# Two column blocks of the latent branch's output projection as a pair with seven-product units, and the last sums in another place

## The chip, the cores and the metric

The kernel runs on one core of one Trainium2 chip. The metric is the time of one execution in device microseconds (us). Five engines work side by side, each through its own queue of instructions, in order: TensorE (PE, matmuls), VectorE (DVE), ScalarE (ACT), GpSimd (POOL) and SyncE (SP). SP and POOL issue the transfers between the chip's memory (DRAM) and the core's own; a transfer is issued by one instruction and lands later.

## The reference

One layer of a decoder on x of 256 tokens x 2048 columns, all float32:

```python
h = rms_norm(x, norm_mix_pre)
c_q, c_kv, k_r, q_s, k_s, v_s, gates = split(h @ w_in)
o_a = mla_attention(...)        # latent attention, 16 heads x 128: 256 x 2048
o_b = swa_attention(...)        # sliding window attention: 256 x 2048
g = sigmoid(gates)              # two gates, 2048 columns each
merged = g[0] * (o_a @ w_o_mla) + g[1] * (o_b @ w_o_swa)
x = x + rms_norm(merged @ w_out, norm_mix_post)
a, b = split(rms_norm(x, norm_ffn_pre) @ ffn_w_up)         # 5632 columns each
c = ffn_conv_b + causal_conv_of_width_3(a, ffn_conv_w)
x = x + rms_norm((gelu(c) * b) @ ffn_w_down, norm_ffn_post)
```

`w_o_mla`, `w_o_swa` and `w_out` are 2048 x 2048. The change concerns `o_a @ w_o_mla` and, in one step, the end of `... @ ffn_w_down`.

## The kernel before, in words

**Precision and tiles.** Every factor is kept as the sum of two parts, high and low. For weights ACT casts the raw tile to the high part (`whi`, L160) and DVE subtracts it from the raw tile for the low part (`wlo`, L161), mostly 128 x 1024 numbers at a time; this is `convert`. A product is three matmuls (`mm3`, L195 to L197): high by high, high by low, low by high. The 256 tokens are two token tiles of 128, the inner dimension goes in k tiles of 128, the columns in blocks of 512. The converted weights turn over in a ring of four tiles, the raw ones in a ring of three and some extra buffers (`more_raw`).

**Blocks and pairs.** `gemm` makes one block of 512 columns. `pair_gemm` makes two blocks, 1024 columns, in units of two k tiles. A unit is eight products for two token tiles, two k tiles and two column blocks; `p` in its order string is such a plain unit. `s` is a unit of seven products, which needs four sums of the activations (token sums, from `token_sums`) and four differences of the weights (weight sums). Some of its products go to four further accumulators (`q1`, `q5`, `q7`, `q6`), and `end_sums` adds these up behind the last `s` into a buffer (`ud`), which is added to the blocks at the end.

**Parked weight sums.** `park_sums` makes the weight sums early: POOL loads two half megabytes of weights to a staging tile, DVE makes four differences (L249), and POOL stores two half megabytes to DRAM (L254, L259). The staging tile is a single one at a time. `seven_parked` loads them later as if they were weights. Units of the down-projection are parked in this way during the latent attention (`tc`, then one of `ta`).

**Steps.** `at(t, f)` enters a step for tick t, and `tick()`, called at each chunk of a product, runs what is due. So ticks count chunks of TensorE's work, and a step's place in the program follows from the tick. A scheduler then orders the instructions and puts the waits.

**Around the change.** The latent attention runs along with the gate of the latent branch, whose last chunk ends it. The gate's values (`ta`, made by ACT at L1005) are stored to DRAM (`ta_d`, L1006). Memory of the attention's pool is given to a new pool (`p6`) behind it. Then come the four column blocks of `o_a @ w_o_mla` (activations `bhl` for its 16 k tiles, accumulators `accg`): each is multiplied with its gate, read back from `ta_d` (`lta`), and gets the other branch's part (`lyb`) added. The result is transposed (`m_cols`) for the pair of `w_out` (accumulators `cw`). The x tiles for the residual are loaded in the meantime (`late_loads`). The token sums for the pair of `w_out` are made in `m_sums`, with weight sums from tiles `mr1hi`, `mr1lo`.

At the kernel's end the down-projection's pairs `db` and `dc` (accumulators `cdc`, `zb` for the last 512 columns in two halves) run; `dsum` (`ds`) holds the sums so far, `ud2` (tiles `ue`) the sums of the pair before, and `z_block` adds the last accumulator and applies the norm.

Of the kernel before, what the change touches and what calls it, by code (L numbers as in the profile page):

```python
# [11 lines left out]
F32 = mybir.dt.float32  # L12
F32R = mybir.dt.float32r
# [3 lines left out]
ALU = mybir.AluOpType  # L17
AX = mybir.AxisListType

P = 128  # L20
D = 2048
S = 256
NT = 2
KT = D // P
# [18 lines left out]
def trunk_layer(ctx, tc, x, x_cols_in, conv_cols_in, g_mix_post, g_ffn_post, w_in, w_q, w_kv,  # L43
# [16 lines left out]
    def sb(pl, shape, name, dt=F32, tag=None, bufs=None):  # L60
        return pl.tile(shape, dt, name=name, tag=tag or name, **({"bufs": bufs} if bufs else {}))
# [14 lines left out]
    def warm_up(n):  # L76
        for i in range(n):
# [6 lines left out]
                       base=0, channel_multiplier=1)  # L84
# [43 lines left out]
    def wchunk(src, shape, own=None, rawp=None, rbufs=1, parts=None):  # L128
        i = cnt[0]
        cnt[0] += 1  # L130
        n = int(np.prod(shape))
        raw = rawp.tile([P, 1024], F32, name=f"raw{i}", tag="xraw", bufs=rbufs) if rawp else \
            new_raw(f"raw{i}")
        dst = raw[:, :n]
        if len(shape) == 2:
            dst = dst.rearrange("p (a b) -> p a b", a=shape[0])
        elif len(shape) == 3:
            dst = dst.rearrange("p (a b c) -> p a b c", a=shape[0], b=shape[1])
        if len(shape) == 3:
# [7 lines left out]
        return convert(raw, n, own=own, parts=parts)  # L147

    def convert(raw, n, own=None, parts=None, into=None):
        i = cnt[0]  # L150
        cnt[0] += 1
        if into:
            hi, lo = into
        elif own:
            hi, lo = (own.tile([P, 1024], F32R, name=f"w{part}{i}", tag="w" + part) for part in ("hi", "lo"))
        else:
            extra = in_turn("w")
            hi, lo = (ring_tile("w" + part, f"w{part}{i}", F32R, extra) for part in ("hi", "lo"))
        for a, b in parts or ((0, n),):
            act.copy(hi[:, a:b], raw[:, a:b])  # L160
            vec.tensor_tensor(lo[:, a:b], raw[:, a:b], hi[:, a:b].bitcast(F32), op=ALU.subtract)  # L161
        return hi, lo
# [14 lines left out]
    def at(t, *fs):  # L177
        steps[max(t, now[0])].extend(fs)
# [711 lines left out]
    def mla_unit(u, t0):  # L890
# [151 lines left out]
    def merge_loads(j):  # L1042
# [6 lines left out]
            ld.append((a, b))  # L1049
        return ld  # L1050

    yg_all = [[sb(p6, [P, 1024], f"yg_{t}_{j}", tag="f" + "ab"[t], bufs=2) for j in range(2)] for t in range(NT)]
    yg = [[yg_all[t][j // 2][:, (j % 2) * 512:(j % 2 + 1) * 512] for j in range(4)] for t in range(NT)]
    ms = {}

    def m_sums(u):
        st = sb(px, [P, 1024], f"ms{u}", F32R, tag="w" + ("hi", "lo")[u % 2])
        ms[u] = token_sums(mt[u].bitcast(F32), yg[0][0], yg[0][1], st[:, 0:512], st[:, 512:1024])

    for i in range(4, 12):  # L1060
        at(now[0] + 10 + 2 * i, lambda i=i: late_loads(i))
    for j in range(4):
        ld = merge_loads(j)
        if j == 2:
            for u in range(W_ORDER.count("s")):
                at(now[0] + 2 + 4 * u, lambda u=u: m_sums(u))
        acc, _ = gemm(AH, AL, wo_a, 0, KT, 512 * j, 512, ps=(pss, "s") if j == 3 else None)
        for t in range(NT):
            a, b = ld[t]
            vec.scalar_tensor_tensor(a, a, 1.0, acc[t], op0=ALU.add, op1=ALU.mult)  # L1070
            vec.tensor_tensor(a, a, b, op=ALU.add)
        for p in range(2):
            at(now[0] + (2 if j == 3 else 1) + p, lambda p=2 * j + p, ld=ld: m_cols(p, ld))


    blocks = [(0, 512), (512, 512), (1024, 512), (1536, 256), (1792, 256)]
# [269 lines left out]
        xl = lambda k: GL(k - k0)  # L1346
        return gemm(xh, xl, w_down, k0, nk, c0, n, split=split, ps=ps)

    def turn_flex(kind):
        flex[0] = kind  # L1350
        turn.update(raw=0, w=0)

    f_raw = lambda n: lambda name: sb(p6, [P, 1024], name, tag="f" + n, bufs=2)

    def deep_raws():
# [111 lines left out]
        ud2[:] = [x_[:, j * 512:(j + 1) * 512] for x_ in (a_tile(f"ue{k}", k) for k in (4, 5)) for j in range(2)]  # L1467
        return ud2

    for i in range(4):  # L1470
        t, j = divmod(i, 2)
        at(now[0] + 16 + i // 2, lambda t=t, j=j, i=i: vec.tensor_tensor(dsum[t][2 + j], dsum[t][2 + j], ud2[i], op=ALU.add))
    at(now[0] + 17, lambda: act.activation(first, ssz[1][:, 1:2], AF.Sqrt))
    more_raw[:] = [raw_of, f_raw("a"), raw_of, f_raw("b"), raw_of, f_raw("a"), raw_x, f_raw("b")]

# [38 lines left out]


RING = 4
GATE_ORDER = "psppspsp"
B_ORDER = "psspsspssp"
B2_ORDER = "ppsspssppp"
# [3 lines left out]
EARLY = 4  # L1523
# [76 lines left out]
```

## Time and profile before

| | |
|---|---|
| time, median of 3 runs | 1459.63 us (1459.4 to 1460.73) |
| profiled execution | 1461.47 us, span 1459.4 us |
| PE busy | 1447.8 us, 99% of the span, 7531 instructions |
| DVE busy | 1140.4 us, 78% |
| ACT busy | 858.0 us, 59% |
| POOL busy | 107.2 us, 7% |
| DMA | 351.08 MB moved, mean 241 GB/s |

A row of a timeline gives the start, the duration, the engine with the line of the kernel, the operation, the tiles (written from read), and in brackets how long the engine stood idle before it and whose work ended that. Starts are counted from the span's start. The durations of matmuls overlap, since they are pipelined; their pace is the distance of the starts. A row of the waits gives who waited for whom, us in total, how often, and the longest.

### The profile page before, as it was taken

Reading aid. Unit: us, or ns where it says so; the run is one execution under the profiler, and the core shown is the slowest. Engines: PE = TensorE matmul, PEld = TensorE weight load, DVE = VectorE, ACT = ScalarE, POOL = GpSimd, SP = SyncE. Lnnn points to the kernel's source line nnn. Section 1 sums busy time; section 2 is a strip of 40 time slices with the busy share of each in tenths; the row PEclk is TensorE's granted clock in tenths of the full one; section 3 lists DMA queues with packets and bytes.
Section 4 is the critical chain, followed back from the end, with each engine's and each line's share of the span. In section 5 each row is a group of like instructions: output and inputs, shape, how many; then the busy total and the mean of one; then the engine's idle time right before and its main releaser. Section 6 shows DMA issues by size and latency. Waiting matters only on the chain.

```text
span 1459.4 us, 21333 instructions
## 1 busy us (share of the span) xinstructions
PE 1447.8 (99%) x7531; PEld 1235.9 (85%) x7531; DVE 1140.4 (78%) x1990; ACT 858.0 (59%) x1412; POOL 107.2 (7%) x192
## 2 busy tenths in 40 slices
PE   9999999999999999999999999999999999999997
PEld 7888888888898888888888888888888888888886
DVE  7788896766778765768799899876778797876797
ACT  7588864544555654446576565655646565665673
POOL 0011110010000001100000011000000100000000
PEclk9999999999999999999999999999999999999999
DMA  8755376699775769864766888856988988667965
GB/s 295 216 164 169 109 260 188 221 322 293 246 216 176 238 226 345 261 200 168 227 207 209 267 313 299 280 174 210 312 271 267 313 270 292 197 188 252 347 218 195
DMA packets 164199, 351.08 MB, mean 241 GB/s; under 512 B 20555, under 2 KB 31724, under 8 KB 164092
## 3 DMA queue, kind: packets, MB, share of 16 engines
q1 hardware_dynamic: 144480, 280.40, 59.3%
q0 software_dynamic: 19520, 69.27, 14.1%
q8 instruction: 59, 0.97, 0.3%
q14 instruction: 48, 0.39, 0.1%
q10 hardware_dynamic: 92, 0.05, 0.0%
HBM read 318.16 MB, written 31.51 MB: 240 GB/s over the span
## 4 chain that ended last, share of the span: by engine, by line
PE 93%; DMA 3%; DVE 2%; ACT 1%; issue 1%; DVEq 0%; ACTq 0%
PE accg L195 10%; PE accg L197 10%; PE accg L196 10%; PE ub L1293 10%; PE ua L1293 10%; PE ub L1297 5%; PE ua L1297 5%; PE cd L195 2%; PE cd L196 2%; PE cd L197 2%; DVE wlo L161 1%; DMA raw<-in_ffn_w_down_dram 1%; PE cdb L196 1%; DMA raw<-in_w_out_dram 1%; PE mpo L977 1%; PE cdb L195 1%
## 5 line engine op out<-in xcount | busy, mean ns | idle before, releaser
L161 DVE TENSOR_TENSOR wlo<-raw,whi 128x1024 fp32r<-128x1024 f32 (+2 forms) x498 | 587.2, 1190 | 206.7 <-ACT whi L160 198.9
L160 ACT CAST whi<-raw 128x1024 fp32r<-128x1024 f32 (+2 forms) x498 | 505.0, 1024 | 384.4 <-PE accg L197 150.1
L195 PE MATMUL accg<-whi,ahl 128*128 128x512 f32 (+1 forms) x416 | 162.8, 391 | 0.0
L197 PE MATMUL accg<-whi,ahl 128*128 128x512 f32 (+1 forms) x416 | 160.6, 386 | 0.0
L196 PE MATMUL accg<-wlo,ahl 128*128 128x512 f32 (+1 forms) x416 | 159.8, 384 | 0.0
L1293 PE MATMUL ub<-ahl,whi 128*128 128x512 f32 x640 | 154.7, 391 | 0.0
L1293 PE MATMUL ua<-ahl,whi 128*128 128x512 f32 x640 | 154.6, 391 | 0.0
L1293 PEld LDWEIGHTS ub<-ahl,whi 128*128 128x128 f32 x640 | 117.5, 188 | 22.9 <-ACT cc L1185 0.3
L1293 PEld LDWEIGHTS ua<-ahl,whi 128*128 128x128 f32 x640 | 117.5, 188 | 22.7
L195 PE MATMUL accg<-whi,bhl 128*128 128x512 f32 x320 | 125.6, 392 | 0.0
L197 PE MATMUL accg<-whi,bhl 128*128 128x512 f32 x320 | 124.8, 390 | 0.0
L196 PE MATMUL accg<-wlo,bhl 128*128 128x512 f32 x320 | 124.7, 390 | 0.0
L197 PEld LDWEIGHTS accg<-whi,ahl 128*128 128x128 f32 x416 | 78.1, 188 | 15.5
L196 PEld LDWEIGHTS accg<-wlo,ahl 128*128 128x128 f32 x416 | 78.2, 188 | 13.1
L195 PEld LDWEIGHTS accg<-whi,ahl 128*128 128x128 f32 x416 | 78.2, 188 | 12.9
L1297 PEld LDWEIGHTS ub<-ahl,wlo 128*128 128x128 f32 x640 | 82.3, 191 | 3.3
L1297 PEld LDWEIGHTS ua<-ahl,wlo 128*128 128x128 f32 x640 | 82.2, 191 | 3.1
L1297 PE MATMUL ua<-ahl,wlo 128*128 128x256 f32 x640 | 83.7, 283 | 0.0
L1297 PE MATMUL ub<-ahl,wlo 128*128 128x256 f32 x640 | 83.3, 283 | 0.0
L197 PEld LDWEIGHTS accg<-whi,bhl 128*128 128x128 f32 x320 | 60.1, 188 | 12.6
L196 PEld LDWEIGHTS accg<-wlo,bhl 128*128 128x128 f32 x320 | 60.1, 188 | 12.1
L195 PEld LDWEIGHTS accg<-whi,bhl 128*128 128x128 f32 x320 | 60.1, 188 | 12.1
(610 smaller groups left out, 2534.9 us busy)
## 6 DMA issues: line engine op xcount, KB each, us to landing
raw<-in_ffn_w_up_dram SPq DMA_DIRECT2D x142, 512.0 KB, 4.6
raw<-in_w_in_dram SPq DMA_DIRECT2D x105, 512.0 KB, 4.6
raw<-in_ffn_w_down_dram SPq DMA_DIRECT2D x66, 512.0 KB, 5.7
xraw<-in_ffn_w_up_dram SPq DMA_DIRECT2D x34, 512.0 KB, 5.1
raw<-in_w_o_swa_dram SPq DMA_DIRECT2D x32, 512.0 KB, 5.1
raw<-in_w_o_mla_dram SPq DMA_DIRECT2D x32, 512.0 KB, 5.6
raw<-in_w_out_dram SPq DMA_DIRECT2D x26, 512.0 KB, 4.2
ta_s<-in_ffn_w_down_dram POOLq DMA_DIRECT2D x24, 512.0 KB, 6.5
```

Source lines behind the costliest of these rows:

```text
L160: act.copy(hi[:, a:b], raw[:, a:b])
L161: vec.tensor_tensor(lo[:, a:b], raw[:, a:b], hi[:, a:b].bitcast(F32), op=ALU.subtract)
L195: pe.matmul(o, ah, bh, start=start, stop=False)
L196: pe.matmul(o, ah, bl, start=False, stop=False)
L197: pe.matmul(o, al, bh, start=False, stop=stop)
L977: pe.matmul(o, w(t), p_[:, c], start=n == 0, stop=n == 5)
L1293: pe.matmul(acc[i], hi[:, c], hn[p][:, j * 512:(j + 1) * 512], start=p + j == 0, stop=stop)
L1297: pe.matmul(acc[i][:, 0:256], lo[:, c], hn[p][:, j * 512:j * 512 + 256], start=False, stop=False)
```

## The change

Blocks 0 and 1 of `o_a @ w_o_mla` become one `pair_gemm` with the order `ppsspssp`: four seven-product units and four plain ones. The weight sums of the four are parked during the latent attention (`tw`), ahead of the four `tc` parks; a park comes every 5 ticks instead of every 7, and the `ta` park moves behind the new pair, so that 8 parks stand there instead of 5. The token sums (`a_sums`) are made by DVE and ACT while the pair runs, with temporary tiles (`at`) and an extra raw buffer (`araw`) in the new pool `p6`. The gates for block 1 have buffers of their own (`la`, `lb`).

Block 2 is computed in the banks that block 3 had, and block 3 in the others. `m_sums` stands in block 3 alone and `late_loads` come later. At the kernel's end the four sums `dsum += ud2` move from ticks in the pair `dc` to behind it. The helper `turn_flex` is moved up unchanged; this shifts the lines of the helpers by 4 (L161 becomes L165, and so on).

```diff
+    parked_w = [park_sums(f"tw{i}_", wo_a, 2 * i, 0, t0=now[0] + 7 + 5 * i, **STAGE) for i in range(NA_)]
     for i in range(NB2):
-        parked_b2.append(park_sums(f"tc{i}_", w_down, 24 + 2 * i, 1024, t0=now[0] + 7 + 7 * i, **STAGE))
-    parked_a.append(park_a(EARLY, t0=now[0] + 7 + 7 * NB2, **STAGE))
+        parked_b2.append(park_sums(f"tc{i}_", w_down, 24 + 2 * i, 1024, t0=now[0] + 7 + 5 * (NA_ + i), **STAGE))
...
+    def a_sums(u):
+        if u % 2 == 0:
+            as_tiles.append(sb(p3, [P, D], f"as{u // 2}", F32R, tag=f"x2_{u // 2}"))
+        o = u % 2 * 1024
+        tmp = sb(p6, [P, 1024], f"at{u}", tag="f" + "ab"[u % 2], bufs=2)
+        as_[u] = token_sums(at_[u].bitcast(F32), tmp[:, 0:512], tmp[:, 512:1024],
+                            as_tiles[u // 2][:, o:o + 512], as_tiles[u // 2][:, o + 512:o + 1024])
...
+    def a_pair():
+        halves = [sb(p6, [P, 1024], f"l{n}1", tag="f" + n, bufs=2) for n in "ab"]
+        lds = [merge_loads(0), [[x_[:, t * 512:(t + 1) * 512] for x_ in halves] for t in range(NT)]]
+        for t in range(NT):
+            for x_, src in zip(lds[1][t], (ta_d, yb_d)):
+                pool.dma_start(x_, src[1, t])
+        gp = sb(p6, [P, D], "araw", tag="gp")
+        more_raw[:] = [raw_of, raw_x, raw_of, raw_f, raw_of, raw_f, lambda name: gp[:, 0:1024], lambda name: gp[:, 1024:2048]]
+        c = pair_gemm("a", wo_a, 0, 0, A_ORDER, lambda k, t: (AH(k)[:, t * P:(t + 1) * P], AL(k)[:, t * P:(t + 1) * P]),
+                      lambda u: as_[u], 0, ud_place, parked=parked_w)
...
+        def pair_evac(i):
+            t, j = divmod(i, 2)
+            vec.tensor_tensor(ud_a[i], ud_a[i], c[i], op=ALU.add)
+            merged(*lds[j][t], ud_a[i])
...
+    for u in range(NA_):
+        at(now[0] + 3 * u, lambda u=u: a_sums(u))
+    for i in range(4, 12):
+        at(now[0] + 20 + 2 * i, lambda i=i: late_loads(i))
+    turn_flex("raw")
+    a_pair()
+    parked_a.append(park_a(EARLY, t0=now[0] + 11, **STAGE))
...
-    for i in range(4, 12):
-        at(now[0] + 10 + 2 * i, lambda i=i: late_loads(i))
-    for j in range(4):
+    for j in range(2, 4):
         ld = merge_loads(j)
-        if j == 2:
+        if j == 3:
             for u in range(W_ORDER.count("s")):
-                at(now[0] + 2 + 4 * u, lambda u=u: m_sums(u))
-        acc, _ = gemm(AH, AL, wo_a, 0, KT, 512 * j, 512, ps=(pss, "s") if j == 3 else None)
+                at(now[0] + 1 + 3 * u, lambda u=u: m_sums(u))
+        acc, _ = gemm(AH, AL, wo_a, 0, KT, 512 * j, 512, ps=(pss, "s") if j == 2 else None)
...
-    for i in range(4):
-        t, j = divmod(i, 2)
-        at(now[0] + 16 + i // 2, lambda t=t, j=j, i=i: vec.tensor_tensor(dsum[t][2 + j], dsum[t][2 + j], ud2[i], op=ALU.add))
...
     for i in range(8):
         unpark(i // 4, i % 4)
+    for i in range(4):
+        t, j = divmod(i, 2)
+        vec.tensor_tensor(dsum[t][2 + j], dsum[t][2 + j], ud2[i], op=ALU.add)
     z_block(c[0], 2, 0)
...
+A_ORDER = "ppsspssp"
+NA_ = A_ORDER.count("s")
```

DVE's queue at the passage from the latent attention to the first block, before. `mptl` and `bhl` belong to the last head; from `wlo_5978` on the low parts are those of block 0. A name after "waits" is the engine or the transfer queue whose semaphore the instruction waits for: `DMAHW` transfers issued by SP, `DMASW` by POOL.

```order
L161 TENSOR_TENSOR wlo_5978<-raw_5975,whi_5977 128x1024 [waits DMAHW2_49,Activation_49]
L414 TENSOR_TENSOR mptl_0_5847<-ptm_0_5848,mpth_0_5846 128x384 [waits Activation_49]
L414 TENSOR_TENSOR mptl_1_5855<-ptm_1_5856,mpth_1_5854 128x384 [waits Activation_49]
L161 TENSOR_TENSOR wlo_5996<-raw_5993,whi_5995 128x1024 [waits DMAHW3_49,Activation_49]
L414 TENSOR_TENSOR bhl_4163<-mpo_5880,bhl_4163 128x512 [waits Activation_49]
L161 TENSOR_TENSOR wlo_6014<-raw_6011,whi_6013 128x1024 [waits DMAHW4_49,Activation_49]
L161 TENSOR_TENSOR wlo_6032<-raw_6029,whi_6031 128x1024 [waits DMAHW5_49,PE_49,Activation_49]
L161 TENSOR_TENSOR wlo_6050<-raw_6047,whi_6049 128x1024 [waits DMAHW6_49,Activation_49]
```

The same passage now; `tc_s` are the differences of the fourth `tc` park, and `wlo_6016`, `wlo_6043`, `wlo_6061`, `wlo_6079` the low parts for the pair's two first plain units.

```order
L165 TENSOR_TENSOR wlo_6043<-raw_6040,whi_6042 128x1024 [waits DMAHW4_49,Activation_49]
L253 TENSOR_TENSOR tc_s<-tc_s 128x512 [waits DMASW7_49,DMASW1_49,DMASW0_49]
L418 TENSOR_TENSOR bhl_4172<-mpo_5904,bhl_4172 128x512 [waits Activation_49]
L253 TENSOR_TENSOR tc_s<-tc_s 128x512 [waits DMASW2_49,DVE_49]
L253 TENSOR_TENSOR tc_s<-tc_s 128x512 [waits DVE_49] x2
L165 TENSOR_TENSOR wlo_6061<-raw_6058,whi_6060 128x1024 [waits DMAHW5_49,Activation_49]
L165 TENSOR_TENSOR wlo_6079<-raw_6076,whi_6078 128x1024 [waits DMAHW2_49,PE_49,Activation_49]
L378 TENSOR_TENSOR at_6032<-bhl_4165 128x512 [waits DMASW3_49,DMASW1_49,DMASW0_49]
L165 TENSOR_TENSOR wlo_6109<-raw_6106,whi_6108 128x1024 [waits DMAHW6_49,Activation_49]
L381 TENSOR_TENSOR at_6032<-at_6032 128x128 [waits DVE_49]
```

The four differences and the token sums of unit 0 (`at_6032`) have come in between, the first of these with a wait for POOL's transfers, ahead of `wlo_6109`, which belongs to unit 0.

POOL's queue at the same passage, before, up to the stores of the gate:

```order
L259 DMA ta_1_3741<-ta_s 128x1024 [waits DMASW4_49,DMASW0_49,DVE_49]
L242 DMA ta_s<-in_ffn_w_down_dram 128x1024 [waits DMASW7_49,DMASW0_49]
L242 DMA ta_s<-in_ffn_w_down_dram 128x1024
L1047 DMA lta_0_5965<-ta_d 128x512 [waits DVE_49,PE_49]
L1048 DMA lyb_0_5966<-yb_d 128x512
L1047 DMA lta_1_5969<-ta_d 128x512 [waits DMASW5_49]
L1048 DMA lyb_1_5970<-yb_d 128x512 [waits DMASW6_49]
L1047 DMA lta_0_6123<-ta_d 128x512
L1006 DMA ta_d<-ta_0_5931 128x512 [waits Activation_49]
L1006 DMA ta_d<-ta_1_5934 128x512 [waits DMASW1_49,Activation_49]
```

And now, from the second store of the third `tc` park:

```order
L263 DMA tc_1_3745<-tc_s 128x1024 [waits DMASW6_49,DVE_49]
L246 DMA tc_s<-in_ffn_w_down_dram 128x1024 [waits DMASW7_49,DMASW0_49]
L246 DMA tc_s<-in_ffn_w_down_dram 128x1024 [waits DMASW2_49]
L1051 DMA lta_0_5996<-ta_d 128x512 [waits DMASW3_49,DVE_49,PE_49]
L1052 DMA lyb_0_5997<-yb_d 128x512
L1051 DMA lta_1_6000<-ta_d 128x512
L258 DMA tc_0_3746<-tc_s 128x1024 [waits DMASW1_49,DVE_49]
L263 DMA tc_1_3747<-tc_s 128x1024 [waits DMASW2_49,DVE_49]
L1010 DMA ta_d<-ta_0_5958 128x512 [waits Activation_49]
L1010 DMA ta_d<-ta_1_5961 128x512 [waits Activation_49]
```

The gate's two stores now stand behind the two stores of the fourth `tc` park, which wait for DVE.

DVE's queue at the kernel's end, before; the last `wlo` is the one for the last product of the pair `dc`, L1472 are the sums `dsum += ud2`, L1398 is `z_block`.

```order
L161 TENSOR_TENSOR wlo_14290<-raw_14287,whi_14289 128x1024
L356 TENSOR_TENSOR ue_14226<-ue_14226,qdc_14010 128x512
L357 TENSOR_TENSOR ue_14225<-ue_14225,qdc_14010 128x512
L1472 TENSOR_TENSOR ds_7716<-ds_7716,ue_14226 128x512
L1472 TENSOR_TENSOR ds_7715<-ds_7715,ue_14225 128x512
L1472 TENSOR_TENSOR ds_7716<-ds_7716,ue_14226 128x512
L161 TENSOR_TENSOR wlo_14302<-raw_14299,whi_14301 128x1024
L1398 TENSOR_TENSOR ds_7715<-ds_7715,cdc_13917 128x512
```

And now:

```order
L165 TENSOR_TENSOR wlo_14407<-raw_14404,whi_14406 128x1024
L360 TENSOR_TENSOR ue_14347<-ue_14347,qdc_14131 128x512
L361 TENSOR_TENSOR ue_14346<-ue_14346,qdc_14131 128x512
L165 TENSOR_TENSOR wlo_14419<-raw_14416,whi_14418 128x1024
L1534 TENSOR_TENSOR ds_7836<-ds_7836,ue_14346 128x512
L1534 TENSOR_TENSOR ds_7837<-ds_7837,ue_14347 128x512 x2
L1446 TENSOR_TENSOR ds_7836<-ds_7836,cdc_14038 128x512
```

Three of the four sums (the first is further ahead in both) have moved from in front of the last `wlo` to behind it.

More of the change, by code (lines that the diff above doesn't have):

```diff
@@ L147, in wchunk, with turn_flex @@
         return convert(raw, n, own=own, parts=parts)
+    def turn_flex(kind):
+        flex[0] = kind
+        turn.update(raw=0, w=0)
     def convert(raw, n, own=None, parts=None, into=None):
@@ L1050, in merge_loads, with merged, ud_place @@
         return ld
+    as_ = {}
+    as_tiles = []
+    def a_sums(u):
[5 more added lines that the diff above has]
+                            as_tiles[u // 2][:, o:o + 512], as_tiles[u // 2][:, o + 512:o + 1024])
+    def merged(a, b, acc):
+        vec.scalar_tensor_tensor(a, a, 1.0, acc, op0=ALU.add, op1=ALU.mult)
+        vec.tensor_tensor(a, a, b, op=ALU.add)
+    ud_a = []
+    def ud_place():
+        d = sb(base, [P, D], "uda", tag="sg")
+        ud_a[:] = [d[:, j * 512:(j + 1) * 512] for j in range(4)]
+        return ud_a
+    def a_pair():
[8 more added lines that the diff above has]
+                      lambda u: as_[u], 0, ud_place, parked=parked_w)
+        more_raw.clear()
+        turn.update(raw=0)
+        def pair_evac(i):
+            t, j = divmod(i, 2)
+            vec.tensor_tensor(ud_a[i], ud_a[i], c[i], op=ALU.add)
+            merged(*lds[j][t], ud_a[i])
+        for n_, i in enumerate((0, 2, 1, 3)):
+            at(now[0] + n_, lambda i=i: pair_evac(i))
+        for p in range(4):
+            at(now[0] + 3 + p, lambda p=p: m_cols(p, lds[p // 2]))
+    for u in range(NA_):
[5 more added lines that the diff above has]
+    parked_a.append(park_a(EARLY, t0=now[0] + 11, **STAGE))
     yg_all = [[sb(p6, [P, 1024], f"yg_{t}_{j}", tag="f" + "ab"[t], bufs=2) for j in range(2)] for t in range(NT)]
@@ L1347, in down @@
         return gemm(xh, xl, w_down, k0, nk, c0, n, split=split, ps=ps)
-    def turn_flex(kind):
-        flex[0] = kind
-        turn.update(raw=0, w=0)
     f_raw = lambda n: lambda name: sb(p6, [P, 1024], name, tag="f" + n, bufs=2)
```

6 lines of the change are left out of this document (2 added, 4 removed).

## The prediction

> **What bounds the kernel now.** I read the page of the profile first (busy time, then the chain that ended last), then the waits of TensorE, then the timelines of its engines at the two places that the change touches.
>
> ```profile
> span 1459.4 us, 21333 instructions
> PE 1447.8 (99%) x7531; PEld 1235.9 (85%) x7531; DVE 1140.4 (78%) x1990; ACT 858.0 (59%) x1412; POOL 107.2 (7%) x192
> PEclk9999999999999999999999999999999999999999
> PE 93%; DMA 3%; DVE 2%; ACT 1%; issue 1%; DVEq 0%; ACTq 0%
> ...
> PE cdc L196 <- DVE wlo L161: 1.3, 1, 1.3
> PE warm L78 <- DVE ramp L67: 1.1, 1, 1.1
> PE pstrip L445 <- DMA sel<-in_strip_sel_dram: 0.4, 1, 0.4
> PE x2T L1103 <- DVE x L1100: 0.4, 1, 0.4
> ```
>
> TensorE (PE) is busy for 99% of the span at the full granted clock, and it waits four times in all, 3.2 us. So two things move the time: matmuls that go away, at their pace in the stream, and waits that PE gains or loses. Work of VectorE (DVE), ScalarE (ACT) and the DMA counts only where PE comes to wait for it. The pace, at the start of the output projection's first block:
>
> ```profile
> 551.57 0.39 PE L196 MATMUL accg<-wlo,ahl 128*128 128x512 f32 x1
> ...
> 552.70 0.39 PE L195 MATMUL accg<-whi,bhl 128*128 128x512 f32 x1
> ...
> 553.38 0.39 PE L195 MATMUL accg<-whi,bhl 128*128 128x512 f32 x1
> ```
>
> Between the first and the third row, nine consecutive matmuls, lie 8 starts: 1.81 us / 8 = 0.226 us each; the 0.39 is a pipelined duration. The second row, 552.70, is the first matmul of block 0 of the latent branch's output projection. I call this moment T0; the changed pair starts there too.
>
> **1. Matmuls that go: -2.7 us.** A seven-product unit does 7 products of 3 matmuls where a plain one does 8. Four units: 4 x 3 x 0.226 = 2.7 us, on the path, since PE is the bound.
>
> The Trainium skill, "TensorE: Matmul & The Clock Gate", section "Back-to-back issue gap", gives about 131 ns as the sustained spacing at 512 columns; by that the twelve would be worth 1.6 us, an estimate from that page. The rows above, 226 ns, speak against it, and the measurement decides.
>
> **2. Last sums moved behind the last weights: -1.2 us.** The longest wait of PE in the kernel is in the last column block:
>
> ```profile
> 1439.08 0.39 PE L195 MATMUL cdc<-wh,bhl 128*128 128x512 f32 x1
> 1440.79 0.50 PE L196 MATMUL cdc<-wlo,ghl 128*128 128x512 f32 x1 [1.33 <-DVE wlo L161]
> ...
> 1435.39 1.22 DVE L161 TENSOR_TENSOR wlo<-raw,whi 128x1024 fp32r<-128x1024 f32 x1
> 1436.52 0.68 DVE L356 TENSOR_TENSOR ue<-ue,qdc 128x512 f32<-128x512 f32 x1
> ...
> 1437.72 1.89 DVE L1472 TENSOR_TENSOR ds<-ds,ue 128x512 f32<-128x512 f32 x3
> 1439.52 1.22 DVE L161 TENSOR_TENSOR wlo<-raw,whi 128x1024 fp32r<-128x1024 f32 x1
> 1441.57 0.69 DVE L1398 TENSOR_TENSOR ds<-ds,cdc 128x512 f32<-128x512 f32 x1 [0.83 <-PE cdc L197]
> ...
> 1433.31 1.06 ACT L160 CAST whi<-raw 128x1024 fp32r<-128x1024 f32 x1 [0.48 <-DMA raw<-in_ffn_w_down_dram]
> ...
> 1450.40 0.42 DVE L1398 TENSOR_TENSOR z<-ds,zb 128x256 f32<-128x256 f32 x1 [0.39 <-PE zb L197]
> ```
>
> PE waits 1.33 us for the low half of the last weights, which stands on DVE behind three last sums; its high half has been cast since 1434.4. In the changed order that subtraction is ahead of the three sums, so it can start at 1437.72 and ends by 1438.9. PE wants it at 1440.79 - 1.33 = 1439.46. The wait goes. The sums then run from about 1438.9 to 1440.7, and the next DVE step, which needs PE's c[0], waited 0.83 us before and now finds it about 1.3 us earlier (1440.2): DVE is some 0.5 us late there, and recovers, since it idles 0.39 us at 1450.40 for PE's last block. Gain 1.0 to 1.33; I take 1.2.
>
> **3. The start of the pair: +5.0 us, the term that decides.** Unit costs for DVE, back to back: 1024 columns 1.13 us (1435.39 to 1436.52 above), 512 columns 0.60 (three in 1439.52 - 1437.72 = 1.80), 128 columns 0.20:
>
> ```profile
> 606.51 0.29 DVE L377 TENSOR_TENSOR yg<-yg 128x128 f32<-128x128 f32 x1
> 606.72 0.29 DVE L378 TENSOR_TENSOR yg<-yg 128x128 f32<-128x128 f32 x1
> ...
> 502.71 0.54 POOL L259 DMA_DIRECT2D tc<-tc_s  x1 [4.13 <-DVE tc_s L249]
> 506.25 1.06 POOL L242 DMA_DIRECT2D ta_s<-in_ffn_w_down_dram  x2 [3.00 <-DMA tc<-tc_s]
> ...
> 535.11 0.54 POOL L259 DMA_DIRECT2D ta<-ta_s  x1 [2.38 <-DVE ta_s L249]
> 540.17 1.08 POOL L242 DMA_DIRECT2D ta_s<-in_ffn_w_down_dram  x2 [4.52 <-DMA ta<-ta_s]
> ...
> 553.21 1.23 POOL L1006 DMA_DIRECT2D ta_d<-ta  x2 [2.85 <-ACT ta L1005]
> ...
> 559.17 0.34 SPq L1029 DMA_DIRECT2D x<-in_x_dram  x1
> ...
> SPq L1029 <- DMA ta_d<-ta: 2.7, 1, 2.7
> ...
> 538.47 0.29 DVE L952 TENSOR_TENSOR mp<-mp,ms 128x128 f32<-128x128 f32 x1
> ...
> tc_s<-in_ffn_w_down_dram POOLq DMA_DIRECT2D x8, 512.0 KB, 6.2
> raw<-in_w_o_mla_dram SPq DMA_DIRECT2D x32, 512.0 KB, 5.6
> ```
>
> The tiles of the token sums (`at`) and the extra raw buffer (`araw`) lie where the latent attention's staging tiles lay, so they may be written only after the stores that read those tiles, the last of which are the two `ta_d` stores of the gate. The kernel before has that wait too: the first load of x, in the same memory, went out at 559.17, released by the `ta_d` store, 6.5 us after T0. There nobody needs x soon. In the changed order the token sum at_6032 has this wait on DVE, with every weight subtraction of the seven-product units behind it, and the load of araw has it on SP's queue.
>
> When do the stores land (S)? Before: issued 553.21 and about 553.8, landed 559.17. After the change POOL's queue first holds the two stores of the fourth down-projection park. Its loads wait for the third park's second store. That one's sum stands on DVE ahead of the row at 538.47, so it is issued at about 539.1. From such a store to the load that it releases passed 3.54 us (502.71 to 506.25) and 5.06 us (535.11 to 540.17), mean 4.3; I take the loads at 543.4 and, with the issue of the second 0.5 us later and 6.2 us, their landing at 550.1. Four sums and one other subtraction of 0.60 each end at 553.1, the park's last store is issued by 553.7, the `ta_d` stores by 554.9 instead of 554.4. With the same 5.4 us from the second issue to landing S is T0 + 7.0; and 1 MB more now goes ahead of them:
>
> ```profile
> 550.00:555.00 5.00, 5.00 (x24) 4.14 (x23) 1.66 (x2) 3.36 (x4) 1.44 (x3) 1.00 0.97 346
> 555.00:560.00 5.00, 5.00 (x24) 4.14 (x23) 2.58 (x3) 2.11 (x2) 0.46 (x1) 1.00 0.82 305
> 570.00:580.00 10.00, 10.00 (x46) 8.23 (x45) 7.21 (x8) 3.44 (x4) 1.09 (x2) 1.00 1.05 392
> ```
>
> The last two columns of a stretch are the DMA engines' busy share and GB/s. At 346 GB/s that megabyte takes 3.0 us, if nothing overlaps: S is T0 + 7.0 to T0 + 10.0; middle T0 + 8.5.
>
> What PE has meanwhile: four chunks of plain work, 48 matmuls, 10.8 us, whose subtractions stand ahead of the wait. What DVE must do from S until the low half of unit 1's second weight sums (wlo_6194): six subtractions of 1024 (6.8), nine operations of 512 (5.4), thirteen of 128 (2.6), and about 0.9 of waiting for araw (5.6 us of load and 1.05 of cast, against 5.7 of DVE work ahead of it): S + 15.7. PE wants that half after 85 matmuls of the pair, at T0 + 19.2. The wait of PE, added up over units 0 and 1, is therefore S - T0 - 3.5: 3.0 us if S is as before (T0 + 6.5), 6.5 at T0 + 10.0, and 5.0 at the middle. I take 5.0. No work hides it: DVE is the engine that is late, and PE has nothing else queued. Later units have a plain unit between and DVE catches up.
>
> **4. The staging in the latent attention: +0.4 us.** Three parks more, at 5 ticks instead of 7: 12 sums of 0.60 = 7.2 us on DVE. None of PE's four waits above lies in the latent attention, so cover exists; a load that comes late would hold DVE for at most about 1 us (store to load 4.3, load 6.2, against 5 ticks). 0 to 1.3; I take 0.4, nearer the end without a wait.
>
> **5. The blocks behind the pair: +0.5 us.** Block 3 now takes the banks which W_out's pair needs in its seventh matmul (1.4 us in), and the block's final sums on DVE stand behind the weight sums from mr1hi:
>
> ```profile
> 614.61 0.69 DVE L227 TENSOR_TENSOR yg<-mr1hi 128x512 f32<-128x512 f32 x1 [2.59 <-DMA mr1hi<-in_w_out_dram]
> 642.37 1.28 DVE L1070 SCALAR_TENSOR_TENSOR lta<-lta,accg 128x512 f32<-128x512 f32 x2
> 642.66 0.39 PE L195 MATMUL cw<-whi,ahl 128*128 128x512 f32 x1
> ```
>
> Before, those sums met PE's start of the W_out pair within 0.3 us, and DVE's wait for mr1hi lay 28 us earlier. The bound is 0 if mr1hi is there, about 3 if the 2.6 us wait now falls at that place; I take 0.5.
>
> **Sum.** -2.7 - 1.2 + 5.0 + 0.4 + 0.5 = +2.0 us. The profiled execution took 1461.47 us (span 1459.4 and 2.1 around it): 1463.5 for such a one. It is 1.84 us above the median of the three runs, 1459.63; on that footing 1461.6. One measurement of this kernel can tell about 0.2%, 2.9 us, from no change.
>
> **The rivals.**
> *The covers hold (faster).* If the `at` tiles' wait is over when DVE comes to it, that is if S is at most T0 + 3.5, terms 3 to 5 are zero: -3.9 us, 1455.7. For it: PE has 10.8 us of plain work first, and the other pairs of this kernel start without a listed wait. Against it: 559.17 shows the stores landing at T0 + 6.5 with less in front of them. Half of it (a DVE order that is less tight than I count) is the same case. Chance 0.18.
>
> *The DMA engines become the limit in the pair (slower).* The pair loads 22 half megabytes and its gates eight quarters, 13.6 MB in 41 us, 332 GB/s; the stretches quoted ran at 305 to 392, one of them at a share of 1.05. At 392 there is room, at 305 it takes 44.6 us, 3.6 more than PE has: +2.0 + 3.6 = +5.6, 1465.2. It decides from under 332 GB/s. Chance 0.22.
> The Trainium skill, "DMA: Bandwidth & Descriptors", section "Specifications", puts the memory's limit per core at about 358 GB/s; by that, an estimate, the 13.6 MB take 38 us and this case falls away. The 392 of the row is above that limit, and the row at 305 with a share of 0.82 neither confirms nor refutes it.
>
> *The bank handover to W_out (slower).* If mr1hi lands late at block 3, PE waits about 3 us at its pair's seventh matmul: +2.0 + 2.5 = +4.5, 1464.1. For it: the 2.6 us wait of before. Against it: it had been over 28 us ahead of the pair. Chance 0.15.
>
> **How the numbers follow.** The forecast, +2.0, gets 0.45. Its own case runs from 0.0 (term 3 at 3.0, S as before) to +3.5 (term 3 at 6.5), 1459.6 to 1463.1; 0.40 of it lies within the 2.9 us, 0.05 above. Slower is that 0.05 and the two slower rivals, 0.42; faster 0.18. The range takes in the forecast's case, most of the faster rival and the slower ones up to the price of the DMA rival: 1456.0 to 1466.0.
>
> **What would show it.** Twelve matmuls fewer in PE's count; no wait of PE at the last wlo, while DVE's last sums stand behind it. In PE's waits new ones at `ca` and `qa`, lines 199 to 201, for DVE's as and wlo, 3 to 7 us in all, the first some 11 us behind the pair's start; before them DVE waits at L378 for the store `ta_d`, and SP at araw. If DVE's wait is there and PE's isn't, the cover was larger than I counted; if PE waits in units 2 and 3 for raw, it is the DMA; if at `cw`, the banks. The prediction is wrong if the time falls by over 3 us, or if the waits at `ca` are under 2 us.

## The result, and the profile after

The changed kernel takes 1475.88 us (median of 5 runs, 1474.45 to 1479.33), the kernel before 1460.25 us on the same chip. The ratio is 1.0111, 95% interval 1.0096 to 1.0125: slower by some 15.6 us, where the prediction said 1461.6, within 1456 to 1466. The profiled execution has a span of 1474.6 us, 15.2 more than that of before.

The page, the same lines as before the change:

```profile
span 1474.6 us, 21437 instructions
PE 1449.3 (98%) x7519; PEld 1234.8 (84%) x7519; DVE 1168.4 (79%) x2046; ACT 869.1 (59%) x1425; POOL 115.6 (8%) x208
```

TensorE has its twelve instructions fewer (7519 for 7531) and yet is busy for 1.5 us more; that is the first hint that some of its matmuls ran slower. Its waits:

```profile
PE cw L199 <- DVE lta L1068: 9.3, 1, 9.3
PE ptm L629 <- DVE mp L967: 2.1, 1, 2.1
PE qa L200 <- DVE wlo L165: 1.8, 2, 1.3
PE warm L78 <- DVE ramp L67: 1.1, 1, 1.1
PE ca L199 <- ACT as L417: 0.8, 1, 0.8
PE mT L1043 <- DVE ahl L421: 0.4, 1, 0.4
PE ca L201 <- DVE as L418: 0.4, 1, 0.4
PE qdc L200 <- DVE wlo L165: 0.4, 2, 0.2
```

The 1.3 us at the last wlo are gone. One wait of 9.3 us, at `cw` (the start of W_out's pair), is most of the loss; the waits at `ca` and `qa` are at the place foretold for the start of the changed pair, though those at `ca` come to 1.2 us only; the one at `ptm` is in the latent attention.

Where the 15.2 us lie follows from the first matmuls of five tiles in the two traces. Each row of this view is one instruction with its count, its duration in ns (shortest, median, longest), and the starts of the first and last of them:

```profile
L199 PE MATMUL cw<-whi,ahl x46: 389/389/796, 647.3 to 700.8; 128*128 128x512 f32 x46
...
L1155 PE MATMUL x2T<-ident,x x32: 270/272/332, 740.5 to 761.6; 128*128 128x128 f32 x32
...
L199 PE MATMUL cdb<-whi,bhl x28: 389/389/389, 1362.8 to 1407.0; 128*128 128x512 f32 x28
...
L199 PE MATMUL zb<-whi,ghl x6: 278/283/283, 1464.0 to 1465.8; 128*128 128x256 f32 x6
```

and, of the kernel before,

```profile
L1103 PE MATMUL x2T<-ident,x x32: 270/272/328, 724.4 to 745.5; 128*128 128x128 f32 x32
...
L195 PE MATMUL cdb<-whi,bhl x28: 388/389/397, 1347.0 to 1391.6; 128*128 128x512 f32 x28
...
L195 PE MATMUL zb<-whi,ghl x6: 278/283/283, 1449.1 to 1450.9; 128*128 128x256 f32 x6
```

| stretch | before, us | after, us | difference | predicted |
|---|---|---|---|---|
| start to T0 (552.70, now 554.72) | 552.7 | 554.7 | +2.0 | +0.4 (term 4) |
| T0 to W_out's pair (642.66, now 647.35) | 90.0 | 92.6 | +2.7 | -2.7 + 5.0 = +2.3 (terms 1 and 3) |
| W_out's pair to x2T | 81.7 | 93.2 | +11.4 | +0.5 (term 5) |
| x2T to the pair db | 622.6 | 622.3 | -0.3 | 0 |
| db to zb | 102.1 | 101.2 | -0.9 | -1.2 (term 2) |
| zb to the end | 10.3 | 10.6 | +0.3 | 0 |

**The start of W_out's pair.** POOL, DVE and TensorE, timelines of the changed kernel:

```profile
629.82 1.14 POOL L1052 DMA_DIRECT2D lyb<-yb_d  x2 [13.90 <-DVE lta L1069]
633.89 0.54 POOL L258 DMA_DIRECT2D ta<-ta_s  x1 [2.94 <-DVE yg L384]
634.43 0.53 POOL L327 DMA_DIRECT2D mr1lo<-in_w_out_dram  x1
636.43 0.54 POOL L263 DMA_DIRECT2D ta<-ta_s  x1 [1.48 <-DVE ta_s L253]
636.96 0.53 POOL L327 DMA_DIRECT2D mr3lo<-in_w_out_dram  x1
637.48 0.54 POOL L1051 DMA_DIRECT2D lta<-ta_d  x1
638.02 0.53 POOL L326 DMA_DIRECT2D mr1hi<-in_w_out_dram  x1
...
652.78 0.69 DVE L231 TENSOR_TENSOR yg<-mr1hi 128x512 f32<-128x512 f32 x1 [9.30 <-DMA mr1hi<-in_w_out_dram]
...
657.47 1.27 DVE L1068 SCALAR_TENSOR_TENSOR lta<-lta,accg 128x512 f32<-128x512 f32 x2
...
658.20 0.80 PE L199 MATMUL cw<-whi,ahl 128*128 128x512 f32 x1 [9.33 <-DVE lta L1068]
...
662.63 0.42 PE L200 MATMUL cw<-wlo,ahl 128*128 128x512 f32 x1
```

The load of mr1hi went out at 638.02, 9.3 us ahead of the pair, because it stands in POOL's queue behind loads that wait for block 2's sums and behind the stores of the moved `ta` park. Why the scheduler put it behind mr1lo, mr3lo and a load of block 3 as well, no run here shows. Before, it went out 35 us ahead:

```profile
607.70 0.54 POOL L322 DMA_DIRECT2D mr1hi<-in_w_out_dram  x1
```

It then took 14.7 us to land, against 6.9 before, as the list of DMA issues from 625 to 660 has it (the last column is us to landing),

```profile
mr1hi<-in_w_out_dram POOLq DMA_DIRECT2D x1, 512.0 KB, 14.7
```

in a stretch in which the DMA engines had no room left (share and GB/s are the last two columns, the granted clock the one before):

```profile
640.00:645.00 5.00, 5.00 (x24) 4.14 (x23) 3.48 (x5) 2.77 (x4) 0.00 (x0) 1.00 0.97 372
645.00:650.00 5.00, 3.87 (x18) 2.86 (x16) 0.00 (x0) 1.97 (x2) 1.05 (x2) 1.00 1.02 372
650.00:655.00 5.00, 0.00 (x0) 0.00 (x0) 2.22 (x4) 0.00 (x0) 0.00 (x0) 0.74 0.77 305
655.00:660.00 5.00, 1.80 (x4) 1.50 (x5) 5.00 (x8) 0.00 (x0) 0.00 (x0) 0.50 0.48 138
```

On DVE the four weight differences made from mr1hi and mr1lo stand ahead of block 3's last sums (L1068), and these free the banks that the pair's seventh matmul needs. After the wait the matmuls start 0.43 us apart instead of 0.226: ten from 658.20 to 662.63, 4.43 us for 2.26. So the place cost 9.3 + 2.2 = 11.5 us, the +11.4 of the table.

### The profile page after: what moved, and what is told of

Same layout as the page of the kernel before. It is cut to its first block, busy times and chain, and to the rows that moved or that the text cites. A ratio compares the mean times of both kernels' runs of the same rounds, so it can differ in the third digit from the quotient of the medians.

```text
span 1474.6 us, 21437 instructions
## 1 busy us (share of the span) xinstructions
PE 1449.3 (98%) x7519; PEld 1234.8 (84%) x7519; DVE 1168.4 (79%) x2046; ACT 869.1 (59%) x1425; POOL 115.6 (8%) x208
## 4 chain that ended last, share of the span: by engine, by line
PE 85%; DVE 6%; DMA 4%; issue 3%; ACT 2%; POOL 0%; DVEq 0%; ACTq 0%; POOLq 0%
PE ua L1345 10%; PE ub L1345 10%; PE accg L199 8%; PE accg L201 8%; PE accg L200 8%; PE ub L1349 5%; PE ua L1349 5%; PE cd L200 2%; PE cd L201 2%; PE cd L199 2%; DVE wlo L165 2%; DMA mr1hi<-in_w_out_dram 1%; DMA tc_s<-in_ffn_w_down_dram 1%; PE cw L199 1%; PE cdb L200 1%
## 5 line engine op out<-in xcount | busy, mean ns | idle before, releaser
L165 DVE TENSOR_TENSOR wlo<-raw,whi 128x1024 fp32r<-128x1024 f32 (+2 forms) x500 | 587.5, 1186 | 172.8 <-ACT whi L164 165.5
L199 PE MATMUL accg<-whi,bhl 128*128 128x512 f32 x256 | 100.7, 393 | 0.0
L201 PE MATMUL accg<-whi,bhl 128*128 128x512 f32 x256 | 99.9, 390 | 0.0
L200 PE MATMUL accg<-wlo,bhl 128*128 128x512 f32 x256 | 99.8, 390 | 0.0
L201 PEld LDWEIGHTS accg<-whi,bhl 128*128 128x128 f32 x256 | 48.1, 188 | 10.0
L200 PEld LDWEIGHTS accg<-wlo,bhl 128*128 128x128 f32 x256 | 48.1, 188 | 9.6
L199 PEld LDWEIGHTS accg<-whi,bhl 128*128 128x128 f32 x256 | 48.1, 188 | 9.6
```

Of the source, the lines that this page charges most:

```text
L199: pe.matmul(o, ah, bh, start=start, stop=False)
L200: pe.matmul(o, ah, bl, start=False, stop=False)
L201: pe.matmul(o, al, bh, start=False, stop=stop)
```

## The experiments

The theory: the late landing of mr1hi, in that order on DVE, makes the 11.4 us. Rivals: block 3's new banks alone; the DMA engines, which would shift the wait to another load. The second question is whether the loss at the pair's start follows the stores as term 3 said. The changed kernel was timed in a job of its own; set against the kernel before of each job, the gains given below over the changed kernel are some 0.4 us smaller.

**The last sums alone.** The kernel before, with the four sums behind the pair `dc`.

```diff
-        at(now[0] + 16 + i // 2, lambda t=t, j=j, i=i: vec.tensor_tensor(dsum[t][2 + j], dsum[t][2 + j], ud2[i], op=ALU.add))
...
+        vec.tensor_tensor(dsum[t][2 + j], dsum[t][2 + j], ud2[i], op=ALU.add)
```

> The kernel before with one edit, the four last sums behind the pair dc. The prediction's term 2 says: the wait of 1.33 us of TensorE at the last wlo goes, -1.0 to -1.3 us, ratio 0.9992. The rival, read from the two traces: the passage from the pair db to the end became only about 0.6 us shorter, with two waits of 0.2 us at qdc, so -0.6 us, ratio 0.9996.

1458.69 us against 1459.89, ratio 0.9992 (0.9983 to 1.0001): -1.2 us, though the interval touches no change. The wait at the last wlo is gone in its profile, and DVE's rows stand as foretold:

```profile
1436.02 1.22 DVE L161 TENSOR_TENSOR wlo<-raw,whi 128x1024 fp32r<-128x1024 f32 x1
1437.15 1.89 DVE L1486 TENSOR_TENSOR ds<-ds,ue 128x512 f32<-128x512 f32 x3
```

**The ta park later.**

```diff
-    parked_a.append(park_a(EARLY, t0=now[0] + 11, **STAGE))
+    parked_a.append(park_a(EARLY, t0=now[0] + 36, **STAGE))
```

> The changed kernel with the ta park 25 ticks later, in the blocks of W_out, nothing else. If the park's two stores and its four differences hold back the load of mr1hi: mr1lo goes out at about 631 instead of 634.4, mr1hi at 632 instead of 638.0, with 1 MB less in front; it lands at 640 to 643, the wait of 9.3 us at cw falls to 0 to 1, the 2 us of halved clock behind it go too, and the time falls by 8 to 11 us. If the banks given to block 3 are the cause by themselves, the wait at cw stays above 5 us and the time falls by under 3.

1469.21 us, ratio 1.0063 (1.005 to 1.0077), 6.7 us faster than the changed kernel. mr1hi went out at 632.80, DVE waited 3.3 us for it, and TensorE at cw:

```profile
PE cw L199 <- DVE lta L1068: 1.2, 1, 1.2
```

So 8.1 us of the wait went with the park, and the stretch from W_out's pair to x2T took 83.9 us, 9.3 less than in the changed kernel. The profiled execution, 1466.87 us, is 9.7 us faster, as expected, although the loss at the pair's start was 3.2 us larger in it (S at T0 + 11.8, below). The median of the four executions fell by 6.7 only, short of 8 to 11; it is the only one of them with a trace, so where the rest lies isn't shown.

**mr1hi early.** Two loads put behind the pair, in place of those at their old place.

```diff
+    mr1 = [sb(px, [P, 1024], f"mr1{n}", tag="w" + n) for n in ("hi", "lo")]
+    for k_, x_ in enumerate(mr1):
+        tc.keep_in_program_order(pool.dma_start(x_, w_out[0 * 2 * P + k_ * P:0 * 2 * P + (k_ + 1) * P, 0:1024]))
...
```

> The changed kernel with the loads of mr1hi and mr1lo issued right behind the pair (ahead of block 2), the ta park and the banks left as they are. If the late landing of mr1hi, ahead of block 3's last sums in DVE's queue, is the whole cause: no wait at mr1hi, the wait at cw falls under 1 us, no drop of the clock there, 10 to 11.5 us faster than the changed kernel (1464 to 1466). If block 3's banks are the cause by themselves, the wait at cw stays above 5 us. If the DMA engines are what is short, the wait turns up at another load of the W_out pair (raw, mr3hi) and the gain is under 6 us.

1463.87 us, ratio 1.0024 (1.0015 to 1.0033): 12.0 us faster than the changed kernel, half a microsecond more than the most expected, with block 3's banks and the ta park as they were. The load goes out right behind the pair's own, DVE no longer waits for it, and at cw there remains

```profile
564.75 0.53 POOL L1113 DMA_DIRECT2D mr1hi<-in_w_out_dram  x1
...
PE cw L199 <- DVE lta L1072: 0.8, 1, 0.8
```

The first row is of POOL's timeline, the second of TensorE's waits. The stretch from W_out's pair to x2T took 82.5 us in its profile, 10.7 less than in the changed kernel, where the kernel before has 81.7. Neither the banks alone nor the DMA engines explain that; the late load does. Whether a late load would have cost as much with block 3 in its old banks was not run.

**Block 3's sums first.** Two runs keep them ahead of W_out's weight differences on DVE, with the load as late as in the changed kernel. The first marked only the first difference:

```diff
+        tc.keep_in_program_order(vec.tensor_tensor(ta[:, a], even[:, b], even[:, a], op=ALU.subtract))
...
+                tc.keep_in_program_order(vec.scalar_tensor_tensor(lt, lt, 1.0, acc[t], op0=ALU.add, op1=ALU.mult))
```

> The changed kernel with block 3's last sums kept ahead of the weight sums from mr1hi in DVE's order; the loads stay as they are. If the bank wait is only the order on DVE: the wait of 9.3 us at cw goes; mr1hi still lands near 652, the weight sums and their casts follow until about 658, and TensorE's first seven-product unit wants them 10.9 us behind the pair's start, at 658: 0 to 2 us of wait there, 9 to 11 us faster than the changed kernel. If the late load hurts in any order: a wait at cw or its further banks of more than 4 us stays, gain under 6.

1473.61 us, ratio 1.0095 (1.0081 to 1.0109). The second difference (L232), which also reads mr1hi, still stood ahead, DVE waited there for 8.8 us, and TensorE 7.1 at cw: this run tells nothing of the order. The second run keeps all four differences behind the sums:

```diff
...
-            weight_sums(even, odd, ta, tb)
+            weight_sums(even, odd, ta, tb, *([tc.keep_in_program_order] if name == "w" else []))
...
```

> The run with the merge first moved only the first of four weight differences; the second, with the same wait for mr1hi, was still ahead of block 3's last sums, and the wait at cw stayed at 7.1 us. Here all four stand behind those sums, on the changed kernel, with the loads as they are. If the price is the order on DVE together with the late load: the wait at cw falls under 1 us; TensorE has the pair's two plain units, 10.9 us, until it wants mr1's weights, and these, landed at about 652 with 47 to 58 as bounds of need, cost 0 to 3 us: 8 to 11 us faster than the changed kernel, 1465 to 1468. If a late mr1hi costs the same in any order: a wait of over 5 us at cw or qw, gain under 5.

1468.3 us, ratio 1.0057 (1.0043 to 1.007), 7.6 us faster than the changed kernel, a little short of the 8 to 11 expected, and the wait at cw is 2.2 us, not under 1. But it is far from the over 5 us of the rival; the stretch from W_out's pair to x2T fell by 9.3 us. mr1hi went out no sooner (639.61), and yet:

```profile
PE cw L199 <- DVE lta L1125: 2.2, 1, 2.2
```

```profile
652.57 0.69 DVE L1125 SCALAR_TENSOR_TENSOR lta<-lta,accg 128x512 f32<-128x512 f32 x1 [2.37 <-DMA lta<-ta_d]
```

The first is of its waits, the second of its timeline: the wait that is left comes from a quarter-megabyte load for block 3 in the same crowded stretch. So it takes both: the late load, and the place of its readers ahead of the sums that free the banks.

**The start of the pair.** Four runs change what stands ahead of the wait or covers it. Six parks instead of eight:

```diff
-    for i in range(NB2):
+    for i in range(2):
...
-    parked_a.append(park_a(EARLY, t0=now[0] + 11, **STAGE))
+    for i in range(2, NB2):
+        parked_b2.append(park_sums(f"tc{i}_", w_down, 24 + 2 * i, 1024, t0=now[0] + 34 + 6 * (i - 2), **STAGE))
...
-    for i in range(sum(NA) - EARLY - 1):
-        parked_a.append(park_a(i + EARLY + 1, t0=now[0] + 8 + 15 * i // 2, **STAGE))
+    for i in range(sum(NA) - EARLY):
+        parked_a.append(park_a(i + EARLY, t0=now[0] + 8 + 13 * i // 2, **STAGE))
```

The last lines put the ta park into the up-projection, whose parks then come every 6.5 ticks instead of 7.5.

> The changed kernel with six parks in the latent attention instead of eight: the third and fourth tc parks and the ta park come behind the pair of W_out's first blocks. The wait of 2.1 us at ptm (DVE waits for the third tc load) goes. The stores of ta_d have no park ahead of them, so by the prediction's step S falls from T0 + 8.5 to about T0 + 6.5 and the loss at the pair's start from 4.4 to about 2.4 us. With the W_out wait gone as in the run with the ta park late: 13 to 16 us faster than the changed kernel, 1460 to 1463. Rival: the landing of the stores is set by other traffic, S stays at T0 + 8 and the loss at 4 us: 1462 to 1464.

1469.02 us, ratio 1.0062 (1.0045 to 1.0079), not the 1460 to 1463 expected. S fell to T0 + 6.35, the loss fell with it, and the wait at ptm went; but there are new losses at and behind the places to which the parks went: waits of 1.4 and 0.9 us at `ub` and `ua` in the up-projection, 1.6 at x2T, 1.3 at accg, and 1.5 are left at cw. The stretch from W_out's pair to x2T still takes 86.7 us, and that from x2T to the pair db 3.2 us more than in the changed kernel. That the parks cause these waits is likely, but no run tests it.

The order pppssssp on the run with mr1hi early:

```diff
-A_ORDER = "ppsspssp"
+A_ORDER = "pppssssp"
```

> The run with mr1hi loaded early, with the pair's order pppssssp in place of ppsspssp: three plain units, 16.3 us of matmuls, ahead of the first seven-product unit. If what is missing at the pair's start is cover: the loss there falls from 4.9 us to about 2 (the second chunk of the third plain unit stands behind the wait, 0.3 us; DVE's work until the fourth unit, 26.4 us from S, against TensorE's 33.8 from T0: 1.6 us). 2 to 3.5 us faster than the run with mr1hi early. Rival: four seven-product units in a row keep DVE busier than TensorE (6.6 against 4.8 us a unit) and the loss only moves to the third and fourth unit: same time, within 1 us.

1463.15 us, ratio 1.0025 (1.0015 to 1.0034): the same as with mr1hi early. The rival's outcome, but not by its mechanism: the loss stood in the first seven-product unit, as one wait of 2.2 us at qa, and the matmuls behind it ran at half pace (granted clock 0.66 in this stretch):

```profile
575.00:580.00 5.00, 4.98 (x15) 3.91 (x16) 5.00 (x6) 3.50 (x5) 0.00 (x0) 0.66 1.00 365
```

This execution, 1466.46 us, is 3.3 above the median, and it also waited 2.6 us at mT behind the pair; so it shows where this one lost its time, and not why the median stayed.

The fourth tc park in the up-projection, on the run with mr1hi early:

```diff
-    for i in range(NB2):
+    for i in range(NB2 - 1):
...
+    parked_b2.append(park_sums("tc3_", w_down, 30, 1024, t0=now[0] + 8 + 15 * (sum(NA) - EARLY - 1) // 2, **STAGE))
```

> The run with mr1hi loaded early, and with the fourth tc park moved into the up-projection, behind the last ta park, so that no park stands ahead of the gate's stores. By the prediction's step, S falls from T0 + 9.0 to about T0 + 6.4 as in the run with six parks, and the loss at the pair's start from 4.9 to about 2.3 us: 2.6 us faster than the run with mr1hi early. Rival: the extra park in the up-projection costs as much there.

1461.39 us, ratio 1.001 (1.0 to 1.0019), 2.5 us faster than with mr1hi early, near the 2.6 expected, though the two intervals overlap (1.0015 to 1.0033 there); S at T0 + 5.7. Its profiled execution, 1471.57 us, is the slowest of its eleven: from it only the pair's start is read here, and the last section says where its time went. Both together:

> Both together: mr1hi early, the fourth tc park in the up-projection, the order pppssssp. With S at T0 + 6.4 DVE's work ends ahead of TensorE's need at each unit (32.8 against 33.8 us at the last): no loss at the pair's start, 4 to 5 us faster than the run with mr1hi early, so 1458.5 to 1460, ratio to the kernel before 0.999 to 1.000. If only the sums at the end gain and the pair itself gives nothing, it stays at 1460 or above.

1461.47 us, ratio 1.0011 (1.0 to 1.0021): no faster than the park alone, and not the 1458.5 to 1460 expected. The loss at the pair's start fell to 1.4 us, but in its profile 1.7 us at ptm and 1.2 at cw were left. Last, the third tc park moved too:

```diff
-    for i in range(NB2 - 1):
+    for i in range(NB2 - 2):
```

> The candidate: mr1hi early, the order pppssssp, six parks in the latent attention, and the third and fourth tc park behind the last ta park in the up-projection. Against the run with three tc parks in the attention it should lose the wait at ptm (1.7 us in that profile), with the pair's start as there: 1459 to 1460.5, ratio to the kernel before 0.999 to 1.0005. If the parks in the up-projection cost there what they save, 1461 or more.

1459.39 us against 1459.80, ratio 1.0 (0.9991 to 1.0009), as expected. The profiled execution, the fastest of its eleven, has a span of 1455.2 us and hardly a wait of TensorE:

```profile
PE warm L78 <- DVE ramp L67: 1.1, 1, 1.1
PE qa L200 <- DVE wlo L165: 0.6, 1, 0.6
PE acckv L519 <- ACT whi L164: 0.3, 1, 0.3
PE pstrip L453 <- DMA sel<-in_strip_sel_dram: 0.2, 1, 0.2
PE cw L199 <- DVE lta L1072: 0.2, 1, 0.2
```

So the pair can be had without loss, but its gain isn't shown: neither this version nor the last sums alone beats the kernel before beyond its interval.

**Term 3 against the runs.** S - T0 is from the pair's first matmul to the first token sum, and the loss is the pair's length (to block 2's first matmul) less 180 x 0.226 = 40.7 us. For the changed kernel

```profile
554.72 0.39 PE L199 MATMUL ca<-whi,bhl 128*128 128x512 f32 x1
...
563.27 0.69 DVE L378 TENSOR_TENSOR at<-bhl 128x512 f32<-128x512 f32 x1 [5.14 <-issue]
...
599.98 0.39 PE L199 MATMUL accg<-whi,bhl 128*128 128x512 f32 x1
...
SPq L172 <- DMA ta_d<-ta: 4.6, 1, 4.6
```

At the token sum the view names no releaser ("issue"). The last row, of the waits of SP's queue, does: the load of araw, which went out at 563.38, waited for the gate's store `ta_d`; and in the runs with six parks and with three tc parks DVE's row names that store too.

| run, order ppsspssp | S - T0 | loss | S - T0 - 3.5 |
|---|---|---|---|
| the changed kernel | 8.6 | 4.6 | 5.1 |
| ta park later | 11.8 | 7.8 | 8.3 |
| six parks | 6.4 | 2.4 | 2.9 |
| block 3's sums first, one difference | 7.4 | 4.3 | 3.9 |
| mr1hi early | 9.0 | 5.0 | 5.5 |
| three tc parks | 5.7 | 2.5 | 2.2 |
| block 3's sums first, all four | 7.4 | 4.2 | 3.9 |

In the two runs with the order pppssssp and no park ahead of the gate's stores (S at T0 + 6.3) the loss was 1.4 us.

## Why the prediction was wrong

**Term 5 is the step that failed.** It put +0.5 us, with a bound of 3, on the handover of banks to W_out, and the rival that named just this mechanism got 4.5 in all and a chance of 0.15. It measured 11.4; of the 13.2 us by which +2.0 missed the +15.2 of the profile, 10.9 are this term's and 1.6 term 4's. The bound was the length of an old wait for mr1hi, 2.6 us, and the argument against it was that this load had been over 28 us ahead of the pair. Both are facts of the old order. What decides is when the load goes out in the new one, and that stands in POOL's queue: behind the two loads of block 3's `lyb` tiles, which wait for block 2's sums, and behind the two stores of the `ta` park that the change had put there. The working followed POOL's queue with care up to T0 and not beyond. The step that is moved, the ta park, was costed at nothing on the queue that it is moved past. Nor did the term count that a queue of transfers makes the landing longer (14.7 for 6.9 us), or that a long wait halves the clock (2.2 us more).

**Term 3 held, with luck in its size.** S was forecast at T0 + 8.5 and lay at 8.55; the loss at 5.0, and it was 4.6. Its formula follows the loss over seven runs, S from 5.7 to 11.8, within 0.6 us. But in the six profiles with the same eight parks ahead of the pair S lies between T0 + 7.4 and T0 + 11.8, so that it came so near to the forecast in this one is luck.

One of the signs that were to show the prediction wrong did come: the waits at `ca` are 1.2 us, under 2. With those at `qa` they come to 3.0 of the 4.6. The list counts idle time only, and each stop stretches the starts around it too: from 567.26, where the first wait ends, to the next matmul it is 0.34 us instead of 0.226.

**Term 1 held.** The twelve matmuls are gone at 0.226 us each. With term 3 it gives +1.9 for the +2.7 of that stretch. The other 0.8 lies ahead of two starts of mT: between the starts at 617.03 and 617.87, and at 620.90 and 621.34, pass 0.84 and 0.44 us, where 0.226 is the pace. The first holds the wait of 0.4 at mT in the list of waits.

**Term 2 held in size.** -0.9 us in the changed kernel's profile, where 0.4 us of waits at `qdc` are new, and -1.2 alone, for -1.2. In the profiles of the experiments this stretch is 1.8 to 2.2 us shorter than in the one profile of before, so it may be more.

**Term 4 was too small for this execution.** +2.0 us for 0.4, outside its bounds of 0 to 1.3. Over the six profiles with the same eight parks T0 lies 0.3 to 3.7 us later than before, three of them within the bounds. The mechanism was the one named: DVE waited 2.19 and 2.04 us for the third tc park's load, and the softmax behind it came 2.1 us late for TensorE.

```profile
527.67 1.06 POOL L246 DMA_DIRECT2D tc_s<-in_ffn_w_down_dram  x2 [3.51 <-DMA tc<-tc_s]
...
534.57 0.69 DVE L253 TENSOR_TENSOR tc_s<-tc_s 128x512 f32<-128x512 f32 x1 [2.19 <-DMA tc_s<-in_ffn_w_down_dram]
537.31 0.69 DVE L253 TENSOR_TENSOR tc_s<-tc_s 128x512 f32<-128x512 f32 x1 [2.04 <-DMA tc_s<-in_ffn_w_down_dram]
...
544.73 0.98 PE L629 MATMUL ptm<-ident,mp 128*128 128x128 f32 x6 [2.13 <-DVE mp L967]
```

The term took a park's five ticks as time enough without turning them into microseconds at that place. The third park's load could go out only at 527.67, when the second park's last store had landed; DVE came to the first difference at 532.4 (534.57 less the wait of 2.19), 4.7 us later, sooner than the 6.2 us of such a load. With two tc parks instead of four in the attention the wait at ptm went; with three, 1.7 and 3.5 us of it stood in the two profiles.

**The DMA rival** was half right: it named the shortage but looked for it inside the pair. The engines were full there too (0.98 to 1.01 of their time from 560 to 575), and TensorE waited for no raw tile; to go by the shares and the longer landing, they were what made the late load later still. The faster rival, S at T0 + 3.5 or less, occurred in no run.

## What to carry to other kernels

When a change takes work out of a stretch, follow every load that the next stretch needs through its issuing queue in the new order, up to its first reader; how early it was before says nothing. A step that moves behind others holds up what comes after it on each of its queues, here loads behind a store that waits for another engine. And look at what stands behind such a reader on its own engine: here it was the operation that frees the banks, which turned a late operand into a stall of the whole TensorE.

## What the runs showed of the hardware that was not expected

After the 9.3 us without work TensorE's granted clock was 0.50, and its matmuls ran 0.43 us apart for 4.4 us. The Trainium skill, "TensorE: Matmul & The Clock Gate", section "What's actually happening", has the clock halved after an idle window of some 3.4 us and released after as long a busy one, which agrees with this place. By that rule a shorter gap would not halve it. Here a gap of 2.5 us did, in the run with the order pppssssp:

```profile
572.48 0.39 PE L199 MATMUL qa<-whi,as 128*128 128x512 f32 x1
575.02 0.69 PE L200 MATMUL qa<-wlo,as 128*128 128x512 f32 x1 [2.15 <-DVE wlo L165]
```

Behind it eight matmuls start 0.43 us apart, which adds 8 x (0.43 - 0.226) = 1.6 us to the wait of 2.2. Between the start ahead of a wait and the start behind it, 3.0 us at mT in the same run and 3.1 us at ptm in the run with all four differences moved had the same effect. But 2.5 us at ptm in the changed kernel, 2.6 us at cw in the run with all four differences moved and 3.2 us at mT in the run with one difference moved had not. So in these traces the length of a gap between 2.5 and 3.2 us does not decide; what does, no run here shows. A sum of waits leaves this cost out.

Single executions of the changed order spread more than those of before: 1458.68 to 1471.57 us in the run with three tc parks, 1458.02 to 1461.57 for the kernel before in the same job. The slowest of them is the one whose trace was kept. It waited 3.5 us at ptm, for the third tc park's load, and, with mr1hi early, still 4.2 at cw:

```profile
PE cw L199 <- DVE lta L1072: 4.2, 1, 4.2
...
DVE lta L1072 <- DMA lta<-ta_d: 4.5, 1, 4.5
```

The first row is of TensorE's waits, the second of DVE's. Both of TensorE's waits are followed by matmuls at half pace (granted clock 0.50 from 545 to 550 and from 655 to 660). The load that came late at cw is another one, that of block 3's gate, issued at 646.74; in POOL's queue it stood behind a load of the next ta park, which had waited 8.5 us for the stores of the one before. It is the pattern of mr1hi once more. Whether the others above the median lost their time in the same way, no run here shows.
